# Statistics of a norm in two granules, a last tile in column parts, and crossbar transfers for some transposes, in a decoder layer on eight cores

## The chip, the cores and the metric

The program runs on all 8 cores of one Trainium2 chip. Each core takes one of the 8 sequences of the batch, and the cores do not talk to each other. Cores 0 to 3 are die 0, cores 4 to 7 are die 1. Each core has five engines: PE (TensorE, matrix products), DVE (VectorE), ACT (ScalarE), POOL (GpSimd) and SP (SyncE, which here only issues DMA transfers); PSUM is the memory that PE writes to, SBUF (SB) the other one on the core. A "crossbar transfer" is a DMA transfer that transposes on its way. The metric is the device time of the slowest core, in microseconds. Most executions of one kernel agree within 0.3%. Some executions fall into a slower state, in which the cores of one die or of both show a lower granted clock.

Besides the time I use the "mean of the cores": every run lists the span of each of its 8 cores, and I average these over a kernel's fast runs. It is less noisy than the slowest core.

## The reference, cut to what matters

```python
h = layer_norm(concat([meta, x]), ...)            # 16 meta tokens + 2048 positions, 1024 channels
proj = h @ w_in                                   # q_lat 384, kv_lat 128, ... per position
q  = rms_norm(q_lat) @ w_q_up;  kv = rms_norm(kv_lat) @ w_kv_up      # latent attention (A)
o_mla = causal_attention(q_mla, k_mla, v_mla)     # 8 heads of 64
o_fox = causal_attention(fq, fk, fv, cum_log_f)   # forgetting attention (B), 8 heads of 64
merged = g_mla * (o_mla @ w_branch_mla) + g_fox * (o_fox @ w_branch_fox)
h = layer_norm(ALPHA * h + merged @ w_out)        # DeepNorm
h = layer_norm(ALPHA * h + conv_glu_ffn(h))       # d_ff 2816; output without the meta rows
```

There are 17 tiles of 128 positions (the last has 16), in five groups of 4, 3, 3, 3 and 4. Three layer norms are taken per tile.

Of the kernel before, what the change touches and what calls it, by code (L numbers as in the profile page):

```python
# [6 lines left out]
F32 = mybir.dt.float32  # L7
# [19 lines left out]
class Sched:  # L27
    ENGS = ("pe", "act", "dve", "pool", "sp")
    G = 64

# [9 lines left out]
    def _keys(self, ap):  # L40
        t = ap.tensor
        name = t.name
        dims = [tuple(d) for d in ap.ap]
        ck = (name, ap.offset, tuple(dims), str(ap.dtype))
        r = self._gcache.get(ck)
        if r is not None:
            return r
        space = str(ap.space)
        if "PSUM" in space.upper():
            pstride, pcount = dims[0]  # L50
            p0 = ap.offset // pstride if pstride > 0 else 0
            r = tuple(("PSUM", name, q) for q in range(p0 // 32, (p0 + pcount - 1) // 32 + 1))
            self._gcache[ck] = r
            return r
        n = ap.size()
        esz = ap.nbytes() // max(1, n) if n else 4
        if esz == 0:
            esz = 4
        isdram = "DRAM" in space.upper() or "HBM" in space.upper()
        if isdram:  # L60
            fdims = dims
            foff = ap.offset
            qs = (0,)
            G = 4096
        else:
            pstride, pcount = dims[0]
            fdims = dims[1:]
            p0 = ap.offset // pstride if pstride > 0 else 0
            foff = ap.offset - p0 * pstride
            qs = tuple(range(p0 // 32, (p0 + pcount - 1) // 32 + 1))  # L70
            G = self.G
        fdims = [d for d in fdims if d[1] > 1 and d[0] != 0]
        if not fdims:
            ranges = [(foff, foff + 1)]
        else:
            fd = sorted(fdims, key=lambda d: abs(d[0]))
            s0, n0 = fd[0]
            outer = fd[1:]
            cnt = 1
            for d in outer:  # L80
                cnt *= d[1]
            if cnt > 256:
                lo = foff
                hi = foff + sum((d[1] - 1) * d[0] for d in fd) + 1
                ranges = [(lo, hi)]
            else:
                starts = [foff]
                for (s, c) in outer:
                    starts = [b + i * s for b in starts for i in range(c)]
                ln = (n0 - 1) * s0 + 1  # L90
                ranges = [(b, b + ln) for b in starts]
        gs = set()
        for lo, hi in ranges:
            for g in range((lo * esz) // G, (hi * esz - 1) // G + 1):
                gs.add(g)
        r = tuple((name, q, g) for q in qs for g in gs)
        self._gcache[ck] = r
        return r
# [230 lines left out]
class Recorder:  # L329
# [5 lines left out]
    EVERY = (10, 8, 408, 10)  # L335
# [3 lines left out]
    def __init__(self, S):  # L339
        self.S = S  # L340
        self.items = []
        self.state = {}
        self.nt = 0
        self.base = {}
        self.line = None
        self.nkeys = {"sp": 16, "pool": 8, "pc": 8, "out": 4}
        self.pools = []
        self.slow = []
# [203 lines left out]
    def dma(self, eng, out, in_, prio=None, key=None, after=None):  # L552
        it = self._item([(eng, "dma", (), dict(out=out, in_=in_), 570.0 if eng != "pool" else 530.0)], {eng: self._prio(eng, prio)})
# [16 lines left out]
    def order(self):  # L570
        items = self.items
        slow = sorted(self.slow, key=lambda q: q.rank)
        tick = [0, self.EVERY[0]]
# [97 lines left out]
        while ev:  # L671
# [62 lines left out]
            else:  # L734
# [8 lines left out]
                if it.tick and slow:  # L743
                    tick[0] += 1
                    if tick[0] >= tick[1]:
                        q = next((q for q in slow if q.left == 1), None)
                        if q is not None:
                            slow.remove(q)
                            tick[1] = tick[0] + self.EVERY[1 if tick[0] < self.EVERY[2] else 3]
                            q.after = it  # L750
                            q.left = 0
                            q.ready = max(q.ready, st + dur + self.RES[e] + self.SEM["pool"])
                            push(q)
# [8 lines left out]
    def replay(self):  # L762
# [5 lines left out]
        for it, (e, name, args, kw, _d) in self.done:  # L768
            kw = {k: res(v) for k, v in kw.items()}
            if it.dma is not None:  # L770
                it.op = S.dma(e, it.key, kw["out"], kw["in_"], after=it.after and it.after.op)
# [16 lines left out]
FIRST = (("sp", "row", None), ("sp", "x0", None), ("pool", "id", None), ("pool", "lat0", None), ("pool", "lat1", None), ("sp", "x2", 0),  # L788
         ("pool", "lat3", None), ("pool", "lat2", None), ("sp", "x1", None), ("sp", "pp", 0), ("sp", "kv", 1), ("pool", "kf", 0), ("pool", "tri16", 1),
         ("sp", "qr", 2), ("sp", "x3", 1), ("sp", "bf", None), ("sp", "kt0", 2), ("sp", "q0", 3), ("sp", "cs", 1), ("pool", "fv0", 3),  # L790
         ("pool", "fv1", 4), ("sp", "x4", 2), ("sp", "q1", 6), ("pool", "kt1", 6), ("sp", "tri32", 1))
BYACT, HALVES = (1, 2, 3, 13), 1
TRI, RANKS = 0.01, (1.75, 2.0, 3.0, 2.0, 2.0, 2.0)
STEP, DPRE, DATT, DEXP = 0.02, 3, 1, 0
# [12 lines left out]
def build_program():  # L807
# [27 lines left out]
    with contextlib.ExitStack() as es:  # L835
# [46 lines left out]
        RMS = K.slots("rms", [small(8, F32, 64) for _ in range(3)])  # L882
        RCP = K.slots("rcp", [small(8, F32, 64) for _ in range(3)])
# [51 lines left out]
        def first():  # L935
# [39 lines left out]
            K.op("pool", "memset", Vm[:, 16, :, 64:65], 0.0, prio=3)  # L975
# [4 lines left out]
        def ln_stats(xb, rows, eps, s):  # L980

            m = s[:, 12:15]
# [5 lines left out]
            K.op("dve", "bn_aggr", out=m[R, 0:2], in_=s[R, 0:12])  # L988
            K.op("dve", "tensor_scalar", out=s[R, 15:16], in0=m[R, 1:2], scalar1=eps, scalar2=None, op0=ALU.add)
            K.op("pool", "tensor_tensor", out=m[R, 2:3], in0=s[R, 15:16], in1=NEGH[R, 0:1], op=ALU.pow)  # L990
            return m

        def ln_stats_act(xb, rows, eps, s, junk):

            m = s[:, 12:15]
            R = slice(0, rows)
            STATS.append(K.op("act", "activation", out=junk[R, :], in_=xb[R, :], func=AF.Copy, scale=1.0 / 1024, accum_out=m[R, 0:1]))
            K.op("act", "activation", out=junk[R, :], in_=xb[R, :], func=AF.Square, scale=-1.0, bias=m[R, 0:1], accum_out=m[R, 1:2])
            K.op("dve", "tensor_scalar", out=s[R, 15:16], in0=m[R, 1:2], scalar1=1.0 / 1024, scalar2=eps, op0=ALU.mult, op1=ALU.add)
            K.op("pool", "tensor_tensor", out=m[R, 2:3], in0=s[R, 15:16], in1=NEGH[R, 0:1], op=ALU.pow)  # L1000
            return m

        def ln_halves(xb, rows, m, dst):

            R = slice(0, rows)
            for h in range(2):
                C = slice(512 * h, 512 * h + 512)
                K.op("dve", "scalar_tensor_tensor", out=xb[R, C], in0=xb[R, C], scalar=m[R, 0:1], in1=GBe[R, 0, C], op0=ALU.subtract, op1=ALU.mult)
                it = K.op("dve", "scalar_tensor_tensor", out=dst[R, C], in0=xb[R, C], scalar=m[R, 2:3], in1=GBe[R, 1, C], op0=ALU.mult, op1=ALU.add)
            return it  # L1010

        def ln_apply(xb, rows, m, G, B, dst):
# [3 lines left out]
            K.op("dve", "scalar_tensor_tensor", out=xb[R, :], in0=xb[R, :], scalar=m[R, 0:1], in1=G[R, :], op0=ALU.subtract, op1=ALU.mult)  # L1016
            for i, b in enumerate(B):
                C = slice(i * w, i * w + w)
                it = K.op("dve", "scalar_tensor_tensor", out=dst[R, C], in0=xb[R, C], scalar=m[R, 2:3], in1=b[R, :], op0=ALU.mult, op1=ALU.add)
            return it  # L1020

        def to_hT(t, rows, hb, parts=1):
            K.line = "tr"
            pb = K.tile(PSUM, "d")
# [18 lines left out]
        def embed2(t):  # L1043
# [9 lines left out]
            to_hT(t, rows, hb, 2 if t < HALVES else 1)  # L1053

        def latent(t):
# [10 lines left out]
            for (a, b, c) in ((0, 384, 4), (384, 512, 5)):  # L1066
                K.any([("dve", "tensor_scalar", (), dict(out=ln_[:, a:b], in0=pl[:, a:b], scalar1=s[:, c:c + 1], scalar2=None, op0=ALU.mult)),
                       ("act", "activation", (), dict(out=ln_[:, a:b], in_=pl[:, a:b], func=AF.Copy, scale=s[:, c:c + 1]))])
            pb = K.tile(PSUM, "d")
# [11 lines left out]
        def v_fox(t):  # L1081
# [3 lines left out]
            K.copy(Vf[:, t, :, 0:64], pv[:, :].rearrange("p (h d) -> p h d", h=8))  # L1085

        def k_fox(g, p):
# [4 lines left out]
            K.copy(Kf[:, p, c0:c0 + n], pk[:, 0:n], CE)  # L1092
# [112 lines left out]
        for j in range(NJ):  # L1205
# [40 lines left out]
        def heads_out(g, dst, ot):  # L1246

            nq = len(GT[g])
            c0, n = gcols(g)
            pb = K.tile(PSUM, "d")  # L1250
# [3 lines left out]
            return K.copy(dst, p16[:, 0:n], engs=CE)  # L1254

        def k_mla(p, g):
# [4 lines left out]
            for b in range(2):  # L1261
                K.copy(KT[(p % 2) * 2 + b][0:64, c0:c0 + n], pk[64 * b:64 * b + 64, 0:n], CE)

        def q_mla(p, g):
# [4 lines left out]
            for b in range(2):  # L1269
                K.copy(qs[b][0:64, 0:n], pq[64 * b:64 * b + 64, 0:n], CE)  # L1270
# [6 lines left out]
        for s, (p, g) in enumerate([(p, g) for g in range(5) for p in (0, 1)] + [(p, g) for p in (2, 3) for g in range(5)]):  # L1277
# [13 lines left out]
            heads_out(g, omT[:, p, c0:c0 + n], ot)  # L1291
# [29 lines left out]
        def attn_fox(g):  # L1321
# [8 lines left out]
            for p in range(4):  # L1330
# [5 lines left out]
                for b in range(2):  # L1336
                    K.copy(qs[b][64 * b:64 * b + 64, 0:n], pq[64 * b:64 * b + 64, 0:n], CE)
# [6 lines left out]
                heads_out(g, of[:, p, 0:n], ot)  # L1344
            return of

        def merge(g, of):
            c0, n = gcols(g)
            K.line = "c"
            K.base = {"pe": RANKS[4], "": RANKS[5]}  # L1350
            for c in range(8):
# [15 lines left out]
                if c == 1:  # L1367
                    go = it
            for i, t in enumerate(GT[g]):
# [4 lines left out]
                K.dma("sp", xb[R, :], xm[t * 128:t * 128 + rows, :], after=go)  # L1374
                ln_apply(xb, rows, MR[:, t, 12:15], Ge, (Be,), xb)
# [10 lines left out]
                to_hT(t, rows, hb)  # L1386
# [54 lines left out]

        for gs in ((0, 1), (2, 3), (4,)):
# [4 lines left out]
            for j in range(NJ):  # L1447
                w = K.tile(WU)
                K.dma("sp", w.v(), scr_u[j])
# [9 lines left out]
            for g, o in zip(gs, offs):  # L1459
                c0, n = FG[g]  # L1460
                for i in range(n // 128):
# [3 lines left out]
                    K.dma("sp", xb.v(), scr_h2[r0:r0 + 128, :])  # L1465
                    for cg in range(2):
# [66 lines left out]
```

## The kernel before: the parts that the change touches

The kernel is recorded, not written in order. Each operation becomes an item. A list scheduler with a model of the costs decides the order on each engine ("the order"), and a replay then emits the instructions, with a semaphore wait wherever an instruction touches a granule of memory that another engine wrote or read. Both steps use the same granules.

```python
class Sched:
    G = 64                      # bytes of SBUF in one dependency granule; 4096 in DRAM
# ... the scheduler's model of costs, in ns
    RES = {"pe": 165.0, "act": 100.0, "dve": 72.0, "pool": 45.0, "sp": 0.0}
    SEM = {"pe": 145.0, "act": 98.0, "dve": 107.0, "pool": 144.0, "sp": 120.0}
    SLACK = 10.0
        if eng == "pool":
            if kw.get("op") == ALU.pow:
                return 400.0 + 120.0 * n
# ... statistics of a norm: mean and deviation in the same 64 bytes
            m = s[:, 12:15]
            for h in range(2):
                bn_stats(out=s[R, 6*h:6*h+6], in_=xb[R, 512*h:512*h+512])            # DVE
            bn_aggr(out=m[R, 0:2], in_=s[R, 0:12])                                     # DVE: mean, variance
            tensor_scalar(out=s[R, 15:16], in0=m[R, 1:2], scalar1=eps, op0=ALU.add)    # DVE
            tensor_tensor(out=m[R, 2:3], in0=s[R, 15:16], in1=NEGH, op=ALU.pow)        # POOL: deviation ** -0.5
# ... its use
            scalar_tensor_tensor(out=xb, in0=xb, scalar=m[R, 0:1], in1=G, op0=ALU.subtract, op1=ALU.mult)  # DVE
            scalar_tensor_tensor(out=dst, in0=xb, scalar=m[R, 2:3], in1=b, op0=ALU.mult, op1=ALU.add)      # DVE
# ... latents of tile t, and head outputs: turned on PE into PSUM, then evicted
            for c in range(4):
                transpose(out=p16[:, c*128:(c+1)*128], in_=ln_[:, c*128:(c+1)*128], identity=identb)       # PE
            K.copy(latT[:, :, T], p16...)                                                             # ACT or DVE
# ... last stage, per tile: two halves of 512 columns, norm, one output of 512 KB
            for cg in range(2):
                dense(pd, ats, wdn[:, j, cg*512:cg*512+512], 22)
                scalar_tensor_tensor(out=xb[:, cg*512:...], in0=xb[...], scalar=ALPHA, in1=pd, ...)
            m = ln_stats(...); ln_apply(...); K.dma("sp", out[...], xb, key="out")
```

(The helper calls are shortened here; the names are those of the kernel.)

The softmax here doesn't subtract the row's maximum and nothing guards it: scores larger than these inputs give would overflow.

## Time and profile before

The time is 1130.19 us as the median of 40 runs (1129.57 in the 6 that were known at the prediction); the mean of the cores is about 1124.

The first lines are from the page of the slowest core: span, busy time by engine, and two rows of the 40 slices (tenths of busy time; PEclk is the granted clock in tenths).

```profile
span 1126.4 us, 25518 instructions; the slowest of 8 cores (1122.4 to 1126.4 us)
PE 1083.4 (96%) x8322; PEld 621.0 (55%) x8322; DVE 771.7 (69%) x1715; ACT 635.8 (56%) x1400; POOL 108.1 (10%) x196
...
PE   5789999999999999999999999999999999999995
...
PEclk9799999999999999999999999999999999999998
```

PE is busy in every slice but the first few and the last. So every microsecond that PE's stream loses is paid, and other engines count only where PE waits for them. The clock is low only in the second slice and in the last, where PE has no work.

The same core in five stretches (columns as the first line names them):

```profile
core 1: us, PE busy (x) PEld busy (x) DVE busy (x) ACT busy (x) POOL busy (x), PEclk, DMA share, GB/s
0.00:60.00 60.00, 40.18 (x184) 18.35 (x185) 33.89 (x62) 30.36 (x66) 20.95 (x39) 0.86 0.72 164
60.00:100.00 40.00, 35.84 (x319) 20.34 (x318) 38.11 (x113) 33.07 (x85) 9.17 (x13) 1.00 0.37 94
100.00:340.00 240.00, 235.69 (x2620) 151.36 (x2617) 175.70 (x567) 224.85 (x588) 36.84 (x69) 1.00 0.62 111
340.00:700.00 360.00, 357.80 (x3012) 216.30 (x3010) 250.08 (x499) 239.79 (x476) 24.97 (x46) 1.00 0.63 163
700.00:1110.00 410.00, 409.50 (x2178) 212.86 (x2177) 267.43 (x469) 107.76 (x189) 15.61 (x29) 1.00 0.37 116
```

From 340 to 1110 us PE idles for 2.7 us in all. The idle time is in the first 100 us (24.0 us), some 4 us come between 100 and 340 us, and about 12 us are the end, where PE has finished.

The end, from the timeline of the same core (start, duration, instruction, idle time before it and what ended it):

```profile
1114.49 0.69 DVE L185 SCALAR_TENSOR_TENSOR SB<-SB,PS 128x512 f32<-128x512 f32 x1 [2.20 <-PE PS L185]
1115.28 0.69 DVE L185 BATCH_NORM_STATS2 SB<-SB 128x6 f32<-128x512 f32 x1
1116.08 0.21 DVE L185 BATCH_NORM_AGGREGATE SB<-SB 128x2 f32<-128x12 f32 x1
1116.39 0.15 DVE L185 TENSOR_SCALAR SB<-SB 128x1 f32<-128x1 f32 x1
1116.69 0.55 POOL L185 TENSOR_TENSOR SB<-SB 128x1 f32<-128x1 f32 x1 [8.60 <-DVE SB L185]
1117.36 2.69 DVE L185 SCALAR_TENSOR_TENSOR SB<-SB 128x1024 f32<-128x1024 f32 x2 [0.81 <-POOL SB L185]
```

The reader sees the chain of the last norm: add, statistics, aggregate, epsilon, POOL's power, and then two passes of DVE, the first of which waits 0.81 us for the power. DVE is done at 1120.05 us, and the span ends at 1126.4.

Two groups of instructions that the change aims at (busy us and mean ns after the bar):

```profile
L185 PE MATMUL PS<-SB 128*128 128x128 bf16 x541 | 60.5, 224 | 15.7 <-DVE SB L185 8.2 <-ACT SB L185 6.9
...
L185 POOL TENSOR_TENSOR SB<-SB 128x1 f32<-128x1 f32 x48 | 26.5, 553 | 532.1 <-DVE SB L185 532.0
```

### The profile page before, as it was taken

The page shows a single profiled execution, that of the slowest core. Times are in us where ns is not written, and L with a number is a line of the kernel's source. Part 1 is how long each engine was busy: PE and PEld are TensorE (multiplying, and loading weights), DVE is VectorE, ACT ScalarE, POOL GpSimd, SP SyncE. Part 2 cuts the span into 40 slices and gives each one's busy share as a digit, 9 for nine tenths or more (in the row PEclk, how much of TensorE's full clock was granted, in tenths as well). Part 3 has the DMA queues.
Part 4 walks back from the last instruction along what each step waited for, and adds up shares of the span by engine and source line. Part 5 has one row for each costly group of instructions (what it writes and reads, how often), then busy time and mean ns, then how long its engine had stood idle before and what let it go on. Part 6 is the DMA issues. An engine that isn't in the chain of part 4 may idle for free.

```text
span 1126.4 us, 25518 instructions; the slowest of 8 cores (1122.4 to 1126.4 us)
## 1 busy us (share of the span) xinstructions
PE 1083.4 (96%) x8322; PEld 621.0 (55%) x8322; DVE 771.7 (69%) x1715; ACT 635.8 (56%) x1400; POOL 108.1 (10%) x196
## 2 busy tenths in 40 slices
PE   5789999999999999999999999999999999999995
PEld 2345566676564565665665555555456665444442
DVE  4699988754666876657647697666566665567754
ACT  4679999999893694995995344342024442013310
POOL 4212221111100000010000001110000000000000
PEclk9799999999999999999999999999999999999998
DMA  8625457467676586875726639872343222334301
GB/s 185 165 72 122 97 78 122 91 85 143 86 159 151 150 188 159 190 152 116 212 86 202 192 86 257 224 168 85 108 145 111 96 98 73 112 131 150 113 19 57
DMA packets 46641, 147.46 MB, mean 131 GB/s; under 512 B 5569, under 2 KB 8129, under 8 KB 46513
## 3 DMA queue, kind: packets, MB, share of 16 engines
q1 hardware_dynamic: 31026, 115.41, 32.0%
q0 software_dynamic: 15488, 30.42, 19.8%
q8 instruction: 72, 1.18, 0.4%
q14 instruction: 55, 0.45, 0.2%
HBM read 159.07 MB, written 34.67 MB: 172 GB/s over the span
## 4 chain that ended last, share of the span: by engine, by line
PE 89%; DMA 3%; ACT 2%; issue 2%; DVE 2%; POOL 1%; POOLq 0%; DVEq 0%; ACTq 0%; SPq 0%
PE PS L185 89%; ACT SB L185 2%; DMA SB<-scr_u 2%; DVE SB L185 2%; DMA SB<-w_lat 1%; POOL SB L185 1%; POOL SB L188 0%; POOLq L224 0%; DVEq L243 0%; ACTq L243 0%; POOLq L243 0%; SPq L243 0%; POOLq L808 0%
## 5 line engine op out<-in xcount | busy, mean ns | idle before, releaser
L185 PE MATMUL PS<-SB 128*128 128x512 bf16 (+8 forms) x8322 | 1083.4, 291 | 31.0 <-ACT SB L185 12.5
L185 PEld LDWEIGHTS PS<-SB 128*128 128x128 bf16 (+1 forms) x8322 | 621.0, 98 | 492.9 <-issue 88.9
L185 ACT ACTIVATE SB<-PS,SB 128x384 bf16<-128x384 f32 (+6 forms) x619 | 313.5, 615 | 221.0 <-PE PS L185 209.2
L185 ACT ACTIVATE SB<-PS 128x384 bf16<-128x384 f32 (+12 forms) x589 | 244.5, 521 | 53.0 <-PE PS L185 50.3
L185 DVE SCALAR_TENSOR_TENSOR SB<-SB 128x1024 f32<-128x1024 f32 (+6 forms) x180 | 180.9, 1008 | 24.4 <-POOL SB L185 16.4
L185 ACT ACTIVATE SB<-SB 128x384 f32<-128x384 f32 (+4 forms) x147 | 92.5, 634 | 163.1 <-DVE SB L185 162.8
L185 DVE SCALAR_TENSOR_TENSOR SB<-SB,PS 128x512 f32<-128x512 f32 (+2 forms) x146 | 91.0, 625 | 102.6 <-PE PS L185 78.0
L185 DVE SCALAR_TENSOR_TENSOR SB<-PS,SB 128x384 f32<-128x384 f32 (+1 forms) x220 | 140.6, 641 | 27.7 <-ACT SB L185 19.2
L185 DVE TENSOR_TENSOR SB<-PS,SB 128x384 bf16<-128x384 f32 (+10 forms) x241 | 110.8, 465 | 63.5 <-ACT SB L185 53.9
L185 DVE TENSOR_TENSOR SB<-SB 128x128 bf16<-128x128 bf16 (+8 forms) x353 | 87.0, 269 | 49.1 <-ACT SB L185 39.5
L185 POOL TENSOR_TENSOR SB<-SB 128x1 f32<-128x1 f32 (+2 forms) x67 | 42.1, 630 | 597.1 <-DVE SB L185 597.0
L185 DVE BATCH_NORM_STATS2 SB<-SB 128x6 f32<-128x512 f32 (+1 forms) x92 | 63.3, 690 | 8.8 <-DMA SB<-xm 3.9
L185 DVE CAST SB<-PS 64x384 bf16<-64x384 f32 (+5 forms) x83 | 49.3, 595 | 15.6 <-PE PS L185 14.2
L188 POOL DMA_DIRECT2D scr_u<-w_u x44 | 23.1, 526 | 218.7 <-ACT SB L185 208.3
L185 DVE COPY SB<-PS 128x2 f32<-128x2 f32 (+9 forms) x88 | 30.6, 352 | 18.0 <-PE PS L185 17.0
L185 DVE COPY SB<-SB 32x384 bf16<-32x384 bf16 (+2 forms) x80 | 20.1, 262 | 9.9 <-PE PS L185 8.2
L185 DVE RECIPROCAL SB<-PS 128x3 f32<-128x3 f32 (+2 forms) x96 | 16.3, 170 | 8.0 <-PE PS L185 6.6
L188 POOL DMA_DIRECT2D SB<-w_dn x22 | 11.7, 535 | 79.4 <-ACT SB L185 79.4
L185 DVE TENSOR_SCALAR SB<-SB 128x1 f32<-128x1 f32 (+2 forms) x68 | 10.1, 153 | 8.6 <-ACT SB L185 5.8
L188 POOL DMA_DIRECT2D scr_c<-w_c x16 | 8.8, 549 | 32.7 <-ACT SB L185 21.2
L185 DVE BATCH_NORM_AGGREGATE SB<-SB 128x2 f32<-128x12 f32 (+1 forms) x46 | 9.4, 205 | 2.6
L185 POOL MEMSET SB<- 128x1152 bf16 (+8 forms) x17 | 8.3, 615 | 2.2 <-DVE SB L185 2.2
(18 smaller groups left out, 35.3 us busy)
## 6 DMA issues: line engine op xcount, KB each, us to landing
SB<-scr_u SPq DMA_DIRECT2D x66, 512.0 KB, 3.2
SB<-scr_c SPq DMA_DIRECT2D x40, 768.0 KB, 6.4
SB<-xm SPq DMA_DIRECT2D x32, 512.0 KB, 8.0
scr_u<-w_u POOLq DMA_DIRECT2D x44, 256.0 KB, 6.9
scr_h<-SB SPq DMA_DIRECT2D x16, 512.0 KB, 4.3
SB<-scr_h SPq DMA_DIRECT2D x16, 512.0 KB, 4.3
out<-SB SPq DMA_DIRECT2D x16, 512.0 KB, 2.7
scr_c<-w_c POOLq DMA_DIRECT2D x16, 384.0 KB, 5.7
```

The lines of the kernel that those rows point to most:

```text
L185: return self._add(eng, lambda e: getattr(e, name)(*args, **kw), rd, wr)
L188: return self._add(eng, lambda e: e.dma_start(out=out, in_=in_, **kw), [in_], [out], dma_key=key, after=after)
```

## The change

Its intent: take 92 transposes off PE, let the first pass of a norm run while POOL takes the power, and shorten the end. Cut to its core:

```diff
 class Sched:
+    FINE = 6144                  # the first 6144 bytes hold the small tiles
-            G = 4096
+            G = 2048             # DRAM
+            f = 32 if not isdram and hi * esz <= self.FINE else G
-    EVERY = (10, 8, 408, 10)
+    EVERY = ((10, 8), (416, 10))
+    def flip(self, out, in_, prio=None):
+        it = self.dma("sp", out, in_, prio=prio, key="flip", kw=dict(transpose=True))
-FIRST = (... "id", "lat0", "lat1", "x2", "lat3", "lat2" ...)        # order of the first loads
+FIRST = (... "lat3", "id", "lat0", "lat1", "x2", "lat2" ...)
-BYACT, HALVES = (1, 2, 3, 13), 1
-TRI = 0.01;  STEP, DPRE, DATT, DEXP = 0.02, 3, 1, 0
+BYACT, HALVES = (1, 2, 3, 13), 0
+TRI = -0.01; STEP, DPRE, DATT, DEXP = 0.01, 3, 1.5, 0.5
+GO, TAIL = (0, 1, 2, 0), 1
+FLIP_L, FLIP_M, FLIP_F = (4, 17), (0, 0, 0, 1, 1), (0, 1, 0, 0, 0)
...
-            K.op("pool", "memset", Vm[:, 16, :, 64:65], 0.0, prio=3)
+            K.op("dve", "memset", Vm[:, 16, :, 64:65], 0.0, prio=3)
+        def deviation(s, R, eps, n):          # mean at s[n], deviation at s[1]: different 32-byte granules
+            bn_aggr(out=s[R, n:n+2], in_=s[R, 0:n])
+            tensor_scalar(out=s[R, 0:1], in0=s[R, n+1:n+2], scalar1=eps, op0=ALU.add)
+            tensor_tensor(out=s[R, 1:2], in0=s[R, 0:1], in1=NEGH, op=ALU.pow)          # POOL
+            if FLIP_L[0] <= t < FLIP_L[1]:
+                K.flip(latT[:, :, T], ln_.v()); return
+            if (FLIP_M if V is Vm else FLIP_F)[g]:
+                return K.flip(dst..., ot[:, 0:nq, :]...)
+        def tail(xb, a):                      # last tile: columns 0:512, 512:768, 768:1024
+            for i, C in enumerate((slice(0, 512), slice(512, 768), slice(768, 1024))):
+                dense(pd, a, wdn[:, j, C], 22); add ALPHA * xb; bn_stats
+            deviation(s, slice(0, 128), LN_EPS, 18)
+            # then two halves of the subtraction, two halves of the scaling, each half written out
```

Cut: engine preferences for copies, which keep their old values, and switches for variants that are off.

## The prediction

> **What bounds it now.** The page gives PE 1083.4 us busy of 1126.4 (96%). The windows show three stretches: 0 to 130 us, PE busy about 105; 130 to 1114.5 us, idle only 6.2; then 11.9 us of a chain after PE is done. So the kernel is bound by PE's stream, plus a head (25 us idle, 9.7 of it before 20 us, DMA share 0.9 to 1.0, where the first weights land) and a tail. In the head the granted clock also sinks (0.82 in 20 to 40 us, 0.75 in 40 to 60): 512-column matmuls start 425 ns apart there, later 216. By the table of waits PE's head waits end on DVE (11.0 us) and ACT (9.3).
>
> **What the change does, costed.**
>
> 1. Crossbar transposes. Latent tiles 4 to 16: 13 x 4 PE transposes; head outputs: latent attention's groups 3 and 4 (4 pairs x 3 and x 4), forgetting group 1 (4 x 3): 40. Together 92 of 541 PE instructions of the 128x128 form. In the packed stream they start 56 ns apart, so 92 x 56 = 5.2 us. The Trainium skill, "VectorE: DVE Perf Modes", section "The three transpose paths", puts a TensorE transpose at 390 ns: taken as the saving that would be seven times too much; the trace decides. It puts the crossbar at 1309 ns per 128x128; before has no crossbar transfer to compare. 25 PSUM evictions (0.4 to 0.6 us each) go too, which helps ACT (about 94% busy from 130 to 300 us). Price: issue to landing of perhaps 3 to 5 us instead of about 1.5, and SP's in-order queue. The head outputs are used much later; only the latent tiles feed near consumers, and attention can fill in. I credit 4.5 us.
>
> 2. Mean and deviation apart. Today DVE waits about 0.82 us for POOL's power in every norm, since the mean shares a 64-byte granule with it; such waits sum to 16.4 us. After, the first pass (1.3 us) covers the power (0.55 us plus two hops). In the packed middle that is worth nothing; in the head DVE is on the chain (95% busy from 60 to 100 us), perhaps 3 of 17 waits count: 2 us.
>
> 3. Tail. Now: add 0.69, statistics 0.69, aggregate, epsilon, power, 2.69 us of apply, output from about 1120, end 1126.4. After: the last part has 256 columns (estimate 0.43 each for add and statistics, half plus overhead), no wait for the power, output in halves. Saves about 1 us of chain and 1 us of transfer, costs about 0.3 us of PE for 44 narrower matmuls: 1.7 us.
>
> 4. Reordered first loads, other ranks, tile 0 in one piece, staggered loads of the merge, finer DRAM granules: together 3 us in the head, including less time at low clock; least certain.
>
> Engine preferences for copies equal the old ones and the load-ahead list is the full one: nothing.
>
> **Prediction.** 4.5 + 2 + 1.7 + 3 = 11.2 us: about 1118 us, 80% range 1108 to 1127. Faster by over 2%: 0.07; within 2%: 0.91; slower: 0.02.
>
> **What would show it.** PE busy falls by 5 to 6 us, its count by about 70 (92 fewer transposes, 22 more matmuls), the 128x128 form to 449; DVE's waits for POOL from 22 us to under 6; last matmul to end about 10 us; PE's idle time to 130 us about 20.
>
> **What would make it wrong.** Crossbar transfers much slower than other DMA, stalling SP or the latents (PE then waits on DMA between 60 and 200 us); a changed order that moves the idle gaps and the low-clock stretch, up to 8 us either way.

## The result, and the profile after

The changed kernel takes 1134.58 us (median of 20 runs, 1131.44 to 1136.84). The ratio to the kernel before is 1.0038, with a 95% interval of 1.0028 to 1.0048. A ratio here is the mean time of one kernel's fast runs over that of the other's of the same rounds, so not quite the ratio of the medians. The forecast was 1118 us with a range to 1127: the change is slower by 0.4%, and the forecast gain did not come. The mean of the cores over its fast runs is 1128.5, so the loss is in all cores, with a wider spread: the slowest core is 4.4 us above the mean, before 3.4 (mean of the 40 fast runs of the kernel before).

The page of the changed kernel's slowest core (core 7; the page before is of core 1):

```profile
span 1136.3 us, 25407 instructions; the slowest of 8 cores (1124.2 to 1136.3 us)
PE 1084.8 (95%) x8252; PEld 619.5 (55%) x8252; DVE 761.3 (67%) x1694; ACT 637.3 (56%) x1398; POOL 147.1 (13%) x195
...
PE   5799999999899999999999999999999999999995
...
PEclk9899999999899999999999999999999999999998
```

The stretches of the same core:

```profile
0.00:60.00 60.00, 41.01 (x191) 18.98 (x192) 35.20 (x64) 32.77 (x72) 25.29 (x39) 0.91 0.76 172
60.00:100.00 40.00, 37.24 (x314) 20.47 (x312) 38.62 (x110) 33.98 (x86) 11.33 (x13) 1.00 0.46 110
100.00:340.00 240.00, 224.35 (x2419) 141.54 (x2418) 154.28 (x523) 212.23 (x556) 39.70 (x65) 0.98 0.72 108
340.00:700.00 360.00, 357.79 (x3050) 215.41 (x3049) 252.84 (x507) 246.09 (x491) 39.09 (x45) 1.00 0.60 165
700.00:1110.00 410.00, 410.00 (x2197) 214.60 (x2196) 268.29 (x473) 112.26 (x197) 29.34 (x31) 1.00 0.39 119
```

Between 100 and 340 us PE is busy 224.35 us where it was 235.69. It idles there, where it was nearly full before. After 340 us PE is as full as before. Core 7 is the worst case: over the eight cores, PE's idle time between 100 and 340 us rose from 5.8 to 11.0 us in the mean.

The end of the changed kernel. The last line starts beside the DVE line above it:

```profile
1124.51 0.42 DVE L187 SCALAR_TENSOR_TENSOR SB<-SB,PS 128x256 f32<-128x256 f32 x1 [1.44 <-PE PS L187]
1125.04 0.43 DVE L187 BATCH_NORM_STATS2 SB<-SB 128x6 f32<-128x256 f32 x1
1125.57 0.24 DVE L187 BATCH_NORM_AGGREGATE SB<-SB 128x2 f32<-128x18 f32 x1
1125.91 0.15 DVE L187 TENSOR_SCALAR SB<-SB 128x1 f32<-128x1 f32 x1
1125.98 2.73 DVE L187 SCALAR_TENSOR_TENSOR SB<-SB 128x512 f32<-128x512 f32 x4
1126.21 0.92 POOL L187 TENSOR_TENSOR SB<-SB 128x1 f32<-128x1 f32 x1 [7.58 <-DVE SB L187]
```

DVE's chain got shorter, as predicted: from the first add to the last pass it takes 1124.51 to 1128.71 = 4.2 us, before 5.56. But the span ends at 1136.3, still 11.9 us after PE (12.0 before).

POOL's power and PE's groups:

```profile
L187 POOL TENSOR_TENSOR SB<-SB 128x1 f32<-128x1 f32 x48 | 65.0, 1355 | 522.7 <-DVE SB L187 522.6
...
L187 PE MATMUL PS<-SB 128*128 128x128 bf16 x449 | 50.2, 228 | 12.1 <-DVE SB L187 10.3 <-ACT SB L187 1.5
...
L187 PE MATMUL PS<-SB 128*128 128x256 bf16 x108 | 22.4, 272 | 0.0
```

The 128x128 form fell from 541 to 449, just the 92 transposes. POOL's power went from 553 to 1355 ns. A late norm on the same core shows why:

```profile
1107.37 0.15 DVE L187 TENSOR_SCALAR SB<-SB 128x1 f32<-128x1 f32 x1
1107.44 1.28 DVE L187 SCALAR_TENSOR_TENSOR SB<-SB 128x1024 f32<-128x1024 f32 x1
1107.67 1.45 POOL L187 TENSOR_TENSOR SB<-SB 128x1 f32<-128x1 f32 x1 [8.04 <-DVE SB L187]
1109.24 1.28 DVE L187 SCALAR_TENSOR_TENSOR SB<-SB 128x1024 f32<-128x1024 f32 x1 [0.52 <-POOL SB L187]
```

The power starts 0.23 us after the start of the first pass and ends 0.41 us after the pass ends (0.40 to 0.44 us in all 43 such norms of each core), so most of its 0.55 us comes after the pass, and the second pass still waits 0.52 us for it. The chain from the epsilon to the last pass got shorter by 0.5 us only: 1107.37 to 1110.52, where the last norm before took 1116.39 to 1120.05.

No other large group of the page changed its duration in such a way (DVE's passes: 1008 and 1009 ns, ACT's activations: 615 and 615).

The crossbar transfers, first the packets before, then the packets and the issues after (count, and us from issue to landing, median):

```profile
DMA packets 46641, 147.46 MB, mean 131 GB/s; under 512 B 5569, under 2 KB 8129, under 8 KB 46513
```

```profile
DMA packets 59360, 150.46 MB, mean 132 GB/s; under 512 B 18161, under 2 KB 20721, under 8 KB 59233
...
SB<-SB SPq DMA_TRANSPOSE x25, 3.8
```

They add 3.0 MB. The core moves 12,719 packets more than before; by the packet sizes in the trace, 11,776 of them are the crossbar's, of 256 bytes each. One lands 3.8 us after its issue in the median on this core (3.5 to 5.0 on the eight), but the slowest of each core took 13.9 to 18.6 us.

PE's waits on that core (us in total, times, longest):

```profile
PE PS L187 <- DVE SB L187: 12.0, 12, 3.7
PE PS L187 <- ACT SB L187: 9.4, 18, 1.4
PE PS L187 <- issue: 7.8, 4, 4.0
...
PE PS L187 <- DMA SB<-SB: 3.2, 1, 3.2
```

Only 3.2 us are a direct wait for a crossbar transfer. I looked at each idle time of PE from 60 to 340 us for a crossbar semaphore among its waits: on the 8 cores this was 0.3 to 3.5 us of 9.5 to 18.4 us, 2.2 us in the mean. So late latent tiles are a part of the loss, but under half of the idle time that was added. The longest, 4.0 us of "issue", has no wait at all. It ends at 294.95 us, within half a microsecond of a fetch of instructions (8 KB, 294.69 to 295.01). Such a gap, of over 2 us between 279 and 295 us, stands on five of the eight cores (2.4 to 4.0 us); the kernel before has one on three (2.8 to 3.4 us).

**A ledger of PE's time.** For each core I added up the distances from one matmul's start to the next at full speed ("packed": 216 ns for 512 columns, 162 for 384, 56 for 128, 29 for 65, and so on, the medians of the trace), the idle time that the profile reports, and the rest ("slowed": low clock, and short stalls that the pipelined records hide). This is my own sum over all records, mean of the 8 cores of the profiled execution, in us. (It misses the span by up to 0.4 us, mostly the last matmul itself. Two cores lack some 75 records in both kernels, which moves a little from packed to slowed, alike in both.)

```
kernel                     span   start  packed  idle  slowed 0-60  60-100  100-340  340-  end
before                   1124.0     3.0  1045.9  29.2          9.7     3.3     13.7   6.8  12.0
changed                  1128.8     3.0  1040.8  34.1         11.2     2.8     17.1   7.6  11.9
```

The packed stream is 5.1 us shorter. That part of the forecast (5.2) is right. But 4.9 us came back as idle time, 5.2 us as slowed time, and the end gave 0.1. The sum is -5.1 + 4.9 + 5.2 - 0.1 = +4.9, against a measured +4.8 of span.

### The profile page after: what moved, and what is told of

Its sections match the earlier page's. It is cut to its first block, busy times and chain, and to the rows that moved or that the text cites. A ratio compares the mean times of both kernels' runs of the same rounds, so it can differ in the third digit from the quotient of the medians.

```text
span 1136.3 us, 25407 instructions; the slowest of 8 cores (1124.2 to 1136.3 us)
## 1 busy us (share of the span) xinstructions
PE 1084.8 (95%) x8252; PEld 619.5 (55%) x8252; DVE 761.3 (67%) x1694; ACT 637.3 (56%) x1398; POOL 147.1 (13%) x195
## 4 chain that ended last, share of the span: by engine, by line
PE 88%; issue 3%; ACT 3%; DMA 2%; DVE 2%; POOL 1%; DVEq 0%; POOLq 0%; ACTq 0%; SPq 0%
PE PS L187 88%; ACT SB L187 3%; DVE SB L187 2%; DMA SB<-w_lat 1%; POOL SB L187 1%; DMA SB<-SB 1%; POOL SB L190 0%; DVEq L226 0%; POOLq L226 0%; DVEq L245 0%; POOL scr_c L190 0%; ACTq L245 0%; POOLq L245 0%; SPq L245 0%; POOLq L820 0%
## 5 line engine op out<-in xcount | busy, mean ns | idle before, releaser
L187 PE MATMUL PS<-SB 128*128 128x384 bf16 (+9 forms) x8252 | 1084.8, 293 | 39.6 <-DVE SB L187 12.0
L187 ACT ACTIVATE SB<-PS,SB 128x384 bf16<-128x384 f32 (+9 forms) x621 | 312.9, 615 | 216.8 <-PE PS L187 208.7
L187 ACT ACTIVATE SB<-PS 128x384 bf16<-128x384 f32 (+11 forms) x585 | 243.1, 528 | 63.5 <-PE PS L187 59.2
L187 DVE SCALAR_TENSOR_TENSOR SB<-SB 128x1024 f32<-128x1024 f32 (+6 forms) x180 | 181.2, 1009 | 20.9 <-POOL SB L187 11.1
L187 POOL TENSOR_TENSOR SB<-SB 128x1 f32<-128x1 f32 (+2 forms) x67 | 81.3, 1215 | 573.7 <-DVE SB L187 573.4
L187 DVE BATCH_NORM_STATS2 SB<-SB 128x6 f32<-128x512 f32 (+2 forms) x93 | 63.3, 682 | 7.9 <-DMA SB<-xm 3.4
L187 DVE RECIPROCAL SB<-PS 128x3 f32<-128x3 f32 (+1 forms) x96 | 16.5, 172 | 22.3 <-PE PS L187 20.7
L187 DVE COPY SB<-PS 128x2 f32<-128x2 f32 (+10 forms) x65 | 20.6, 322 | 10.8 <-PE PS L187 10.6
L187 DVE BATCH_NORM_AGGREGATE SB<-SB 128x2 f32<-128x12 f32 (+2 forms) x46 | 9.5, 206 | 2.5
L190 POOL DMA_DIRECT2D SB<-w_o x8 | 4.3, 534 | 42.7 <-ACT SB L187 38.1
```

Source lines behind the costliest of these rows:

```text
L187: return self._add(eng, lambda e: getattr(e, name)(*args, **kw), rd, wr)
L190: return self._add(eng, lambda e: e.dma_start(out=out, in_=in_, **kw), [in_], [out], dma_key=key, after=after)
```

## The experiments

Eighteen kernels ran. "Mean" is the mean of the cores less that of the kernel before in the same rounds.

| label | order | granules | crossbar | other | median us | ratio | mean |
|---|---|---|---|---|---|---|---|
| e1 | new constants | fine | none | tail | 1137.15 | 1.0079 | +9.2 |
| e2 | new | fine | latents | tail | 1134.42 | 1.0050 | +5.5 |
| e3 | new | fine | heads | tail | 1131.66 | 1.0024 | +3.9 |
| e4 | new | fine | all, one semaphore | tail | 1132.15 | 1.0031 | +4.4 |
| e5 | old constants, redone | fine | all | tail | 1140.43 | 1.0091 | +8.4 |
| e6 | old constants, redone | fine | none | tail | 1140.49 | 1.0089 | +8.6 |
| e7 | new | coarse | all | tail | 1137.09 | 1.0058 | +4.7 |
| e8 | new | coarse | none | tail | 1134.19 | 1.0044 | +5.6 |
| e9 | held | fine (waits only) | none | | 1131.81 | 1.0018 | +0.8 |
| e10 | held | coarse | none | tail | 1132.22 | 1.0013 | +0.5 |
| e11 | nudged | coarse | none | | 1133.61 | 1.0039 | +3.7 |
| e12 | old constants, redone | coarse | all | | 1134.35 | 1.0037 | +2.3 |
| e13 | held | coarse | all | | 1186.85 | 1.0414 | +45.0 (die 0) |
| e14 | held | coarse | heads | | 1138.20 | none | -2.2 (die 0) |
| e15 | held | coarse | none | tail, deviation on ACT | 1136.19 | 0.9976 | -3.8 (die 0) |
| e16 | nudged | coarse | none | | 1142.81 | 1.0036 | +0.3 (die 0) |
| e17 | old constants, redone | fine | none | tail, model told | 1133.05 | 1.0031 | +3.7 |
| e18 | held | coarse | heads | tail, deviation on ACT | 1125.04 | 0.9968 | -5.0 |

"Held" means that a listing of the instructions shows the same order on every engine as before, but for the instructions that the edit adds or drops. All results were correct. For e13 to e16 the chip had a die 1 that was slower throughout, for the kernel before too (1135.5 against 1124.9 for die 0, granted clock 0.979 against 0.989). There I use the mean of cores 0 to 3 over all runs; one run of e14, in which that die fell to 1193, is left out.

### First batch: is it the crossbar?

My first theory (A) was that the crossbar transfers cost more than they free.

e1 turns all of them back, e2 and e3 keep one kind each, e4 puts all on one semaphore:

```diff
-FLIP_L, FLIP_M, FLIP_F = (4, 17), (0, 0, 0, 1, 1), (0, 1, 0, 0, 0)
+FLIP_L, FLIP_M, FLIP_F = (99, 0), (0, 0, 0, 0, 0), (0, 0, 0, 0, 0)     # e1
+FLIP_L, FLIP_M, FLIP_F = (4, 17), (0, 0, 0, 0, 0), (0, 0, 0, 0, 0)     # e2
+FLIP_L, FLIP_M, FLIP_F = (99, 0), (0, 0, 0, 1, 1), (0, 1, 0, 0, 0)     # e3
-        self.nkeys = {..., "flip": 8}
+        self.nkeys = {..., "flip": 1}                                  # e4
```

> The changed kernel with all 25 crossbar transposes turned back into PE transposes; everything else of the change stays. Theory A (the crossbar transfers cost more than the 5.2 us of PE they free, because the latent tiles land late, up to 18 us, and PE waits from 100 to 340 us): PE's idle time after 100 us falls back to about 8 us per core (from 14 in the changed kernel), the stretch of the very end (SP's drain to the last event) from 5.0 to 3.3 us, and the time is 1121 to 1127 us. Rival B (the new order, first loads and ranks are at fault, crossbar transfers are innocent): the time stays at 1133 us or above, since 5 us of PE work come back.

> Only the 13 latent tiles go over the crossbar, the 12 head outputs are turned on PE again. Theory A, near consumers: almost all of the loss stays, 1133 to 1139 us, with gaps of PE of 1 to 4 us between 100 and 300 us. If the head outputs were the harmful part (SP queue held up by their waits), the time is below 1130 us.

> Only the 12 head outputs go over the crossbar, the latents are turned on PE again. Theory A: as fast as or about 1 to 2 us faster than the kernel with no crossbar transfer (40 x 56 ns = 2.2 us of PE less, no near consumer), minus up to 1.7 us if the longer end belongs to any use of the crossbar. Rival: SP held up, slower than that kernel by over 2 us.

> All crossbar transfers stay, but all on one semaphore, so that each waits for the one before (7 semaphores fewer). Two questions. End of the kernel: if the 1.7 us longer stretch after SP's drain comes of the number of semaphores, it falls from 5.0 to about 3.5 us; if it comes of having used crossbar transfers at all, it stays at 5.0. Contention: if transfers in flight together delay each other, late landings (over 10 us) become fewer and PE idles less; if ordinary traffic delays them, or the wait for the one before is long, the time stays at 1132 to 1140 us.

Measured: 1137.15, 1134.42, 1131.66 and 1132.15 us. Without any crossbar transfer the kernel is not faster but slower, so theory A falls as an account of the whole loss: with these constants the kernel that has the transfers is the faster one by 4.4 us in the mean of the cores, though the list is redone in each of these kernels and not the transfers alone differ. The heads alone are best, 5.3 us under e1 in the mean of the cores, which is more than the 2.2 us of PE that they free. One semaphore instead of eight brings the mean to about that of the changed kernel (+4.4) and the slowest core nearer to it (2.1 us above it). The late landings became fewer, as asked: the slowest of each core took 7.3 to 11.6 us, with eight semaphores 13.9 to 18.6. But PE's idle time hardly fell (33.1 us, in the changed kernel 34.1), so they were not the main loss. The stretch from SP's drain to POOL's first event after its own drain (the "last event" of the expectations), 3.3 us before and 5.0 in the changed kernel, stayed at 4.8 to 5.0 us in all four, so neither the crossbar nor the number of semaphores makes it.

### Second batch: constants or granules?

```diff
-FIRST, BYACT/HALVES, TRI, STEP, DPRE, DATT, DEXP, GO, EVERY = new
+FIRST, BYACT/HALVES, TRI, STEP, DPRE, DATT, DEXP, GO, EVERY = old      # e5; e6 also without crossbar
-    FINE = 6144
+    FINE = 0                                                           # e7; e8 also without crossbar
```

> The changed kernel (crossbar transfers, mean and deviation apart, tail in column parts) with the order constants of before: first loads, tile 0 in halves, ranks and steps, staggering of the merge, pacing. Theory C (the new constants cost about 8 us, most of it as idle and slowed PE before 340 us; the crossbar transfers gain what they free): below 1127 us, about 1124. Theory D (mean and deviation apart is the fault: POOL's power runs beside the DVE and takes 1.2 us instead of 0.6, and the list that orders the work does not know it): stays at 1133 us or more. Also: the stretch from SP's drain to the last event is 5.0 us in all kernels of the change so far, with and without crossbar; it tells nothing about either theory, but shows whether the constants cause it.

> As e5, without crossbar transfers: the kernel before plus mean and deviation apart, tail in parts, finer DRAM granules. Theory C: 1126 to 1130 us, at or a little under the kernel before (tail and granules gain 0 to 3 us). Theory D: 1134 us or more.

> The changed kernel with granules of 64 bytes again in the small region, so that the subtraction of the mean waits for the power as before. All else of the change stays. Theory C: no better than the changed kernel, 1133 to 1138 us. Theory D: 1124 to 1129 us, and POOL's power of one column is back at about 0.6 us from 1.2.

> New constants, 64-byte granules, no crossbar transfer. Theory C: as slow as the kernel without crossbar of the first batch, 1135 to 1139 us. Theory D: 1128 to 1132 us. If it lies between, both parts count, or the order as such moves the time by some us whatever the edit.

Measured: 1140.43, 1140.49, 1137.09 and 1134.19 us. Theory C (the constants) falls: with the old constants the kernel gets worse with the crossbar (e5) and is hardly better without (e6 +8.6, e1 +9.2). Theory D (the split norm) fits only in part: without crossbar, coarse granules gain 3.6 us in the mean (e1 to e8), but with the crossbar they gain nothing (changed kernel to e7). The parts do not add: crossbar transfers are worth -4.4 us in the mean with new constants and fine granules, -0.9 with coarse ones, -0.2 with old constants and fine ones. e6 is the most telling. It is the kernel before with finer granules, the tail and one moved memset, has the same matmuls, and its cores are 8.6 us slower. Its ledger says idle 34.1 (before 29.2) and slowed time 37.5 (before 33.5), and the stream itself is unchanged. Something that is not work had changed: the order, and with it the engine of a few copies, which the list also picks (ACT has 9 instructions more). In a listing of the instructions by engine, about a quarter of e6's rows differ from those of the kernel before, far more than the tail and the memset account for.

### Third batch: the order held

To separate the parts from the order, I made kernels whose order is the old one. For e9 the list is made with 64-byte granules, and only the replay uses 32-byte ones:

```diff
+    FINE = 0                     # while recording and ordering
+        S.FINE = 6144            # for the waits of the replay
+        S._gcache.clear()
         K.replay()
```

e10 adds the tail alone, with 2048-byte granules for the output only. e11 changes one number of the model in the kernel before, and nothing else:

```diff
-    SEM = {"pe": 145.0, ...}
+    SEM = {"pe": 146.0, ...}     # e11
```

e12 is the kernel before with the 25 crossbar transfers alone; the list is redone.

> The kernel before, instruction for instruction in the same order on every engine, only with the statistics laid out and waited for as in the changed kernel (32-byte granules when the waits are made, 64-byte ones when the order is made). It gives the bare effect of mean and deviation apart. Theory E (the order, redone by the list scheduler after each edit, is what moved the time; the parts as such are harmless): 1125 to 1130 us, equal or up to 3 us faster than before. Theory D (the power beside the DVE hurts): over 1133 us. POOL's power of one column should take 1.2 us in either case.

> The kernel before in the same order, only the last tile in column parts (and the output's granules halved, so that its two halves do not wait for each other); the mean still shares its granule. If the tail is worth what was predicted less the wait for the power: 1.0 us faster, 1127 to 1129.5 us. If the stretch after SP's drain, 3.3 us before and 5.0 in every kernel of the change, grows with the tail's extra instructions: it is 5.0 here and the gain is eaten, 1129 to 1131 us; the other suspect for it is the order or the set of POOL's instructions, then 3.3 here.

> The kernel before with one number of the scheduler's own model nudged, the PE's semaphore latency from 145 to 146 ns. No work, tile, wait rule or priority is changed; the list puts about a sixth of its rows elsewhere. Theory E: slower than before by 2 to 10 us (before is the pick of many trials), 1131 to 1140 us. If the order as such does not matter: 1128 to 1131 us.

> The kernel before with the 25 crossbar transfers alone (old constants, granules, tail). The order is redone by the list. Theory E: 5.2 us of PE less, against a new order that costs 2 to 10: 1126 to 1136 us, with PE's stream at full speed 5 us shorter and more idle time and short stalls before 340 us. If crossbar transfers are a gain on their own: about 1125 us.

Measured: 1131.81, 1132.22, 1133.61 and 1134.35 us.

e9: the bare split of the norm costs 0.8 us in the mean, and the end is 0.9 us longer. PE's idle time is 28.7 us (29.2 before). So the split neither hurts nor helps the body while the order is held; the time lies between what the two theories expected. POOL's power still gets slower, in 19 of 67 cases to over 1.2 us on core 1 (44 of 67 in the changed kernel, 2 before); on the slowest core:

```profile
L187 POOL TENSOR_TENSOR SB<-SB 128x1 f32<-128x1 f32 x48 | 42.1, 878 | 517.5 <-DVE SB L187 517.5
```

e6 is the counterpart of e9 and e10: the same split and the same tail, but with the list redone. The parts cost 0.8 and 0.5 us with the order held; e6 costs 8.6. So some 7 us there come with the redone order; finer DRAM granules and the moved memset are the only other differences.

e11: no work, wait rule or priority changed, and the mean is 3.7 us worse. An order that is redone can by itself cost as much as the whole change cost.

e12: the fastest core of the profiled execution is at 1119.4 us and the slowest at 1136.0 (before 1122.4 to 1126.4). The packed stream is 5.1 us shorter, idle time is 6.2 us and slowed time 2.6 us longer.

e10 gained nothing, though DVE's chain got shorter, and here is why. In the trace POOL's closing drain ends 8.91 us after the end of POOL's last power: this holds on all 8 cores of all twenty kernels (8.90 to 8.91; the 8.95 in an expectation below runs to POOL's next record). From the trace, in us:

```
kernel, core        PE end   last power of POOL   POOL's drain ends   last output landed   span ends
before, 1          1114.38   1116.69 to 1117.24             1126.15              1122.78     1126.38
changed, 7         1124.41   1126.21 to 1127.13             1136.03              1130.87     1136.27
```

In the tail's own tile of 96 bytes, mean and deviation lie in different granules even of 64 bytes, so my expectation for e10 was wrong to say that they share one: the power runs beside DVE there too. The output lands 3.6 us (before) and 5.4 us (changed) ahead of the end. The program ends with POOL. The tail's early statistics brought the power forward, its parts made the power run beside DVE and take 0.92 us instead of 0.55, and so the end moved by 0.1 us. The chain of waits of the profile ends with DVE's last pass and does not show this; the drain is not counted as busy.

### Fourth batch: the crossbar with the order held, a second nudge, and the end

For e13 and e14 the list is made with the PE transposes in it; at the replay they are dropped, and the transfer is issued where the eviction stood:

```diff
         for it, (e, name, args, kw, _d) in self.done:
+            if it in self.pin:
+                if self.pin[it] is not None:          # the eviction: a transfer in its place
+                    o, i = self.pin[it]
+                    it.op = S.dma("sp", "flip%d" % (nf % 8), res(o), res(i), transpose=True)
+                    nf += 1
+                continue                              # the PE transposes: dropped
```

e15 is e10 with the last deviation taken off POOL:

```diff
-            deviation(s, slice(0, 128), LN_EPS, 18)
+            pre = activation(out=SDEV[:, 2:3], in_=ones32[:, 0:1], func=AF.Sqrt)   # table, after the last SiLU
+            bn_aggr(out=s[:, 18:20], in_=s[:, 0:18])
+            tensor_scalar(out=SDEV[:, 0:1], in0=s[:, 19:20], scalar1=LN_EPS, op0=ALU.add)
+            activation(out=SDEV[:, 3:4], in_=SDEV[:, 0:1], func=AF.Sqrt)           # ACT
+            reciprocal(out=SDEV[:, 1:2], in_=SDEV[:, 3:4])                         # DVE, after the subtraction
```

e16 is a second nudge: SLACK from 10 to 11.

> The kernel before with its order held: the list is made with the PE transposes in it, and only afterwards the 4 (or 3) PE transposes of each of the 25 turns are dropped and the crossbar transfer put where their eviction stood. So PE has 5.2 us less to do and no other instruction moves. Theory E (the redone order is what costs, not the transfers): mean of the cores below before's 1124.1 by 2 to 5 us. Rival F (the transfers themselves stall PE through latent tiles that land late, unequally from core to core): mean of the cores not below 1123 us, the slowest core over 1130 us, the time 1131 us or more, with gaps of PE of 2 to 6 us between 100 and 300 us.

> The same with only the 12 head outputs turned by the crossbar (40 PE transposes, 2.2 us). Their consumers come late, so both theories expect the 2.2 us in full, and a slowest core no further from the mean than before (3.6 us): 1126 to 1128.5 us. If it is not faster, the transfers cost something even off the chain (SP's queue, DMA traffic).

> The kernel before in its order, tail in column parts, and the last tile's deviation taken off POOL: square root on ACT (its table loaded after the last SiLU), reciprocal on DVE, in a granule of its own. In every kernel and core so far POOL's closing drain ends 8.95 us after the end of POOL's last power, and that, not the landing of the output, ends the program. If that is so, the stretch from PE's end to the last event falls from 12.0 to about 7 us (SP's drain at 6.7 us then ends it) and the time to 1124 to 1126 us. If the drain is tied to the end of the program instead of to POOL's last instruction, the tail stays at 11 us or more.

> A second nudge of the scheduler's model in the kernel before (slack of a wait from 10 to 11 ns), nothing else. Theory E: 1131 to 1140 us again, as the first nudge (1133.6). If the first nudge was an outlier: 1128 to 1131 us.

On die 0 the kernel before is at 1124.9. e14 is at 1122.7: 2.2 us less, what 40 times 56 ns would give (die 0 of one kernel scatters by about 1 us here). e13 is at 1169.9, 45 us more, where theory E asked for 2 to 5 less; rival F had it right. The only difference is the 13 latent tiles, whose consumers the old order has placed close behind. PE's waits of e13 show it:

```profile
PE PS L187 <- DMA SB<-SB: 33.3, 11, 4.3
PE PS L187 <- DVE SB L187: 11.7, 8, 5.4
PE PS L187 <- ACT SB L187: 10.9, 15, 3.2
```

So where a consumer stands near in PE's queue, a landing of 4.6 us (median) stalls everything behind it: 30 to 35 us of such waits on each of the eight cores. And the waits cost more than their length. On die 0 the packed stream is 5.1 us shorter than before, but idle time is 33 us and slowed time 18 us longer. Of PE's 32 gaps of over 2.6 us after 60 us there, 29 had a drop of the granted clock to 0.5, for 3.4 us or more, that began between the start of the gap and 4 us after its end; in the kernel before it was 3 of 3 on the eight cores, in the changed kernel 4 of 6. The list, when redone, moves the consumers away, and then the direct wait shrinks (to 0.3 to 3.5 us in the changed kernel), at the price of another order.

e15 is at 1121.1, 3.8 us less. The end fell from 12.0 to 7.6 us. POOL's drain now follows the power of the tile before (8.91 us after it) and is over 5.0 us before the end on core 1, so the drain belongs to POOL's last instruction, not to the program's end.

e16 is at 1125.2, 0.3 us more on the undisturbed die; the ratio of the times is unclear (0.9995 to 1.0076). My expectation of 1131 us or more cannot be read on this chip, but the mean says that this nudge cost next to nothing. A redone order is thus not always worse. Two nudges, each of which changed about a sixth of the listing's rows, cost 3.7 and 0.3 us.

### Fifth batch: why the order with fine granules is so bad, and a version that gains

e17 is e6 with one number changed in the model of the scheduler:

```diff
             if kw.get("op") == ALU.pow:
-                return 400.0 + 120.0 * n
+                return 1150.0 + 120.0 * n
```

e18 joins e14 and e15.

> The slow kernel with old constants, mean and deviation apart, tail in parts and no crossbar (1140.5 us, mean of the cores 1132.7), changed in one number of the scheduler's model: POOL's power of one column costs 1270 ns there instead of 520, which is what it takes when the DVE runs its first pass beside it (44 of 67 powers in the changed kernel took over 1.2 us). Theory G (finer granules are harmless when the order is held, but the list, once it knows them, plans for a power that is done in 0.5 us and so queues work behind it that stands): the mean of the cores falls by 5 us or more, to 1124 to 1128. If it falls by less than 3 us, theory G is not supported, and the cost is that of a redone order, whatever the reason for redoing it. Between: unclear, since one nudge of the model has cost 0.3 and another 3.7 us.

> The kernel before in its own order with the two parts that gained when the order was held: the 12 head outputs by crossbar (2.2 us on the undisturbed die) and the last tile in parts with its deviation on ACT (3.8 us). If they add up: 6 us under the kernel before, ratio 0.993 to 0.996, tail 7.6 us. It would beat both kernels.

e17: 1133.05 us, and the mean of the cores fell from +8.6 to +3.7, by 5.1 us from 1132.7 to 1127.6. Theory G asked for 5 us or more; each against the kernel before in its own rounds the fall is 4.9, so it stands on the threshold. With nudges worth up to 3.7 us I call the theory supported and not shown: with fine granules the list plans that the power is done in 520 ns beside the first pass, but the chip gives it 1346 ns in the mean of e6 (1454 beside a full pass), and what the list queued behind it stands.

e18: 1125.04 us, ratio 0.9968 (0.9949 to 0.9987), mean of the cores -5.0. It beats both kernels, though the two parts (2.2 and 3.8) did not quite add up to the 6 us and the ratio of 0.993 to 0.996 that I expected. Its page and its end (slowest core, 6):

```profile
span 1121.5 us, 25419 instructions; the slowest of 8 cores (1114.2 to 1121.5 us)
PE 1076.9 (96%) x8229; PEld 619.7 (55%) x8304; DVE 769.0 (69%) x1709; ACT 636.4 (57%) x1402; POOL 107.4 (10%) x195
```

```profile
1107.03 0.55 POOL L187 TENSOR_TENSOR SB<-SB 128x1 f32<-128x1 f32 x1 [8.95 <-DVE SB L187]
...
1115.42 0.23 DVE L187 BATCH_NORM_AGGREGATE SB<-SB 128x2 f32<-128x18 f32 x1
1115.84 0.15 DVE L187 TENSOR_SCALAR SB<-SB 128x1 f32<-128x1 f32 x1 [0.18 <-DVE SB L187]
1115.91 1.40 DVE L187 SCALAR_TENSOR_TENSOR SB<-SB 128x512 f32<-128x512 f32 x2
1116.08 0.20 ACT L187 ACTIVATE SB<-SB 128x1 f32<-128x1 f32 x1 [35.72 <-DVE SB L187]
1117.22 0.16 DVE L187 RECIPROCAL SB<-SB 128x1 f32<-128x1 f32 x1
1117.49 1.41 DVE L187 SCALAR_TENSOR_TENSOR SB<-SB 128x512 f32<-128x512 f32 x2
```

POOL's last power stands at 1107.03, before PE's end at 1114.27. ACT takes the root in 0.20 us under the first passes. The end is 7.3 us in the mean of the cores.

## Why the prediction was wrong, point by point

The forecast added up four gains and gave the redone order no cost. Of the four, only the shorter PE stream came, and idle and slowed time of 10.1 us ate it twice over. What the prediction would look at bears this out: the 128x128 form fell to 449 and PE's count by 70, but PE's busy time did not fall (1083.4 to 1084.8 us, on different cores).

- **What bounds it.** Right: PE's stream, a head and a tail. But "idle only 6.2 us" was read as if no work there could lose time. The ledger shows slowed time of 20.5 us after 100 us even before, and it grew by 4.2.
- **Step 1, crossbar transposes, credited 4.5 us.** The size of the work was right: 5.1 us of packed stream went (the Trainium skill's 390 ns, "VectorE: DVE Perf Modes", "The three transpose paths", would have said 36). With the order held, the heads gave 2.2 us of 2.2. What failed is the sentence "only the latent tiles feed near consumers, and attention can fill in". Engines queue in order, so nothing fills in unless the list puts it there: held, the latents cost some 47 us (e13 against e14), 33.3 us of it in plain waits for the transfers on core 7. The prediction had named such waits as what would make it wrong, and gave them no term. Redone, the transfers alone came to +2.3 us in the mean (e12).
- **Step 2, mean and deviation apart, 2 us.** The step that failed: "the first pass (1.3 us) covers the power (0.55 us plus two hops)". POOL's power runs mostly after that pass: it ends 0.41 us after it and takes 1355 ns in the mean instead of 553. The Trainium skill, "SBUF — State Buffer", section "SBUF: two separate sides", says that DVE and POOL share a pair of ports as an exclusive lock, and names a DVE operation with two SBUF inputs against a POOL operation that reads SBUF. The first pass is one such. The trace agrees (the power that takes 0.55 us alone ends 0.41 us after the pass), though no run tests the ports themselves, and I should have looked it up for the pair that the change overlaps. DVE's waits for POOL fell only from 22.0 to 12.2 us, not under 6. In the held order the split was worth nothing (e9: PE's idle 28.7 against 29.2 us).
- **Step 3, the tail, 1.7 us.** It gave 0.1. The chain of DVE was sized well (5.56 to 4.2 us). The failed step is that the output ends the program. POOL's drain ends it, 8.91 us after POOL's last power. With the deviation off POOL the tail gave 4.4 us of end (e15).
- **Step 4, order and constants, 3 us in the head.** PE's idle to 100 us went from 24.4 to 23.4 us in the mean of the cores, and its slowed time there rose by 1.0: nothing. Here lies the largest omission: the prediction gave "a changed order" up to "8 us either way", but only as a caveat and not as a term of its sum. In the runs a redone order cost 0.3 and 3.7 us after nudges without any work, and some 7 us with fine granules (e6 against e9 and e10).
- **What is left open.** That the redone order made the loss of the changed kernel itself is inferred from e6, e9 to e14 and the nudges; no run holds the old order with all its parts. I did not separate the new constants from the finer DRAM granules, the tail and the moved memset within e8 (+5.6 us). Why one nudge costs 3.7 us and another 0.3 is not traced to single waits; a kernel that was tuned to its order would make most redone orders worse, which the runs fit but do not prove. The gap of PE between 279 and 297 us, 4.0 us on core 7 and there beside a fetch of instructions, is seen and not explained; it also comes in kernels without a crossbar transfer (e8, e9, e10 and e15) and is missing in others with them (e2 to e5).

## What to carry to other kernels

When a scheduler makes the order, hold the old order while testing an edit: only then did each part here show its worth (heads -2.2 us, latents some +47, split norm +0.8, tail +0.5, tail with the deviation off POOL -3.8). Before overlapping two engines, ask whether they share a port; and if they do, correct the scheduler's model too, or it may plan for an overlap that does not come (e17 supports this without showing it). Before shortening the last chain, find the engine whose last event really ends the program; here it was one that the busy times do not show.

## What the Trainium skill lacked or had wrong

- "GPSIMD Engine Reference" gives no cost for the closing drain of POOL; here it ends 8.91 us after the end of POOL's last power, on all 8 cores of twenty kernels, and it decided the end of the program wherever that power stood in the last tile. "VectorE: DVE Perf Modes", section "The DRAIN you can't avoid", speaks of the runtime's own drains, about 12 ns on all five engines at the start and end; the one here carries a line of the program (L224 of the kernel before), lasts 9.48 us there, and is not covered.
- "VectorE: DVE Perf Modes", section "The three transpose paths", gives 390 ns for a PE transpose; in a packed stream they start 56 ns apart, so a saving is to be counted at 56 ns. The same table's 1309 ns for a crossbar transfer is for 128x128; 128x384 and 128x512 took 2.5 to 6.3 us from issue to landing in the median of a core (e2 to e18), and up to 25.0 us at the worst (e14).
- "Advanced Engine Details and Errata", section "X-Bar Transpose (TRN2)", calls crossbar transfers as fast as regular ones; it says nothing of the spread. In the changed kernel the slowest of 25 took 13.9 to 18.6 us, depending on the core, and they move in packets of 256 bytes.
- "SBUF — State Buffer", section "SBUF: two separate sides", agrees with the runs, which add the size for a small operation: a power of one column that starts 0.23 us into a pass of 128x1024 takes 1.45 us instead of 0.55, and the pass is not longer for it.
